# First layer's output projection in seven products of quarters (Strassen's scheme) instead of eight

## The chip, the cores and the metric

The kernel runs on one core of one Trainium2 chip. The metric is the device time in microseconds (us), the median of the runs shown. A core has a matrix engine (TensorE, in the profile PE for the matmul and PEld for loading its stationary operand), a vector engine (VectorE, DVE), a scalar engine (ScalarE, ACT), a general engine (GpSimd, POOL) and one that here only issues DMAs (SyncE, SP). Each engine works through its own list of instructions in the order in which it was built; an instruction that waits for a semaphore holds up all behind it on its engine.

## What is computed

A backbone of two layers over 512 latent tokens and 256 context tokens, 768 together, with 1024 features. Layer 0 mixes the tokens by differential attention with 8 heads, layer 1 by grouped-query attention. Cut to what the change touches, layer 0 ends so:

```python
o = rms_norm(o1 - lam * o2, subln_g) * (1 - lam_init)     # 8 heads of 128 features
y = (o.reshape(S, 1024) * silu(z)) @ w_out[0]               # the output projection
x = x + gate * rms_norm(y, post_g[0])                       # latent tokens; ctx likewise
h = rms_norm(x, pre_g[1]) * (1 + scale) + shift             # input of layer 1: K, V, Q, z
```

Below, g is the gated output of the heads (768 tokens by 1024 features), W is `w_out[0]` (1024 by 1024), and y = g W. W's quarters are W00 (heads 0 to 3, columns 0 to 511), W01 (heads 0 to 3, columns 512 to 1023), W10 and W11 (heads 4 to 7).

## The kernel before, in words

**Matmuls in three terms.** All large products are done in `fp32r` with a high and a low part of each operand: `mm3` (lines 142 to 145) issues high x high, high x low, low x high into one accumulation. An operand of 128 x 1024 weights is made by `wsplit` (line 209): a load of 512 KB into one of two "raw" buffers (line 211), a cast to the high part on ScalarE (line 213), and the difference to the low part (line 207, in `pieces`), on VectorE in one instruction or on GpSimd in four pieces of 256 columns. `WStream` (from line 225) holds the list of all weights in the order of use: a weight is asked for as soon as a slot for its two parts is free, three slots of the pool `wp`, and later one more in the pool `bp`, which lies where head 7's buffers were (`ws.extend`, line 1169). `release` frees a slot and asks for the next in the list.

**The projection.** It runs over column groups `OUTC` (line 267): 0 to 255, 256 to 511, 512 to 1023, with 2, 2 and 4 weight tiles. For each group and each of the six tiles of 128 tokens, `out_proj` (line 404) adds up eight heads of three terms: 24 matmuls with the token tile stationary and 256 or 512 columns of weights moving.

**Order of the work.** `flow` (line 346) merges the attention's steps (scores `S_`, transposes `T_`, probabilities times values `M_`, sub-layer norms `X_`) with a queue `fillq` of projections, by a planner with a cost and a due time for each step. Steps run at a raised priority, which moves their instructions ahead in the engines' lists. For head h, the norm of the head (`subln`) and `z_proj` (line 841) end in `gate_mul` (line 836), which multiplies the head by its gate on GpSimd. The last entry of the queue is `out_early` (line 1076): when seven heads are done, `split_g` (line 1023) makes high and low parts of heads 0 to 6, and the first column group is started on six banks of PSUM with the heads 0 to 6. Head 7 is finished in two parts, tokens 0 to 511 and 512 to 767, by `subln_last` (line 986), with its own gate and split (lines 998 and 999). After it the pool of layer 0 is closed, and the code from line 1165 on places new tiles there; x and the context are loaded again for the residual (lines 1171 and 1174), behind the last reader of those buffers.

The loop at lines 1206 to 1225 adds head 7 to the first group, and does the second; each tile's result is multiplied by the layer's gate (`u0`) on VectorE and squared and summed (`sumsq`) on ScalarE. The last group's loop (1274 to 1284) does the tiles of the third group, and with each of them `resid_a` (line 1230) and `resid_b` (line 1238): the norm of y, the residual and the norm of x. Two tiles later `h1_tr` (line 1255) transposes that tile on TensorE, scales it, and writes the high and low part of layer 1's input h. Then K and V of layer 1 are projected, in an order written out by hand in `KV` (line 44; loop at line 1352): 'k' and 'v' are projections, 't' the transposes of a token tile, 'c' those of K, 'g' parts of layer 1's gate vector, whose loads are `gate1_load` (line 1177). The banks of PSUM are four single ones (`bk`) and two pairs (`sc`).

## Time and profile before

| | |
|---|---|
| time before, median of 3 runs | 825.95 us (825.36 to 826.91) |
| span of the profiled execution | 822.0 us |
| median less that span | 3.95 us |
| TensorE busy in the span | 792.7 us, 96% |
| VectorE, ScalarE, GpSimd busy | 482.3, 457.1, 440.4 us |
| the stretch from 459 to 538 us (head 7's end and the projection): TensorE, VectorE, ScalarE, GpSimd busy | 76.86, 45.30, 41.91, 22.36 us |
| mean granted TensorE clock | 0.992 |

The profile shows one execution. "Busy" is the time in which an engine had an instruction at work; the span goes from the first to the last instruction. The time of a run is taken outside of it and is some microseconds longer. Of the profiled execution the page gives the span only. A row of groups reads: line of the code, engine, operation, output <- inputs, shape, count | busy time, mean in ns of one | idle time of the engine before them and who ended it. A row of waits reads: engine, line <- the one waited for: total us, times, longest.

### The profile page before, as it was taken

How to read it: one execution, taken by the hardware profiler on the slowest of the kernel's cores; microseconds unless marked ns; L12 is line 12 of the kernel's file. 1: busy time of each engine (PE TensorE's matmuls, PEld its weight loads, DVE VectorE, ACT ScalarE, POOL GpSimd, SP SyncE). 2: the span in 40 equal slices, each digit the busy share in tenths (PEclk: the TensorE clock that was granted, in tenths of full speed). 3: DMA queues.
4: the chain of work that ended last, by engine and by line, in shares of the span. 5: the costliest groups of instructions: out<-in, count | busy, mean ns of one | idle time of the engine just before them, and what ended most of it. 6: DMA issues, size and time to landing. Idle time of an engine off the chain costs nothing. (4 is left out here: it accounts for less than half of the span.)

```text
span 822.0 us, 14412 instructions
## 1 busy us (share of the span) xinstructions
PE 792.7 (96%) x5482; PEld 703.0 (86%) x5482; DVE 482.3 (59%) x896; ACT 457.1 (56%) x1001; POOL 440.4 (54%) x538
## 2 busy tenths in 40 slices
PE   7999999999999999999999999999999999999997
PEld 5678897788887898787988898889999899898986
DVE  3425566754768524675458952579546566755534
ACT  6534357664575544765556852674446576666631
POOL 4544766856367744665822311587788656733101
PEclk9999999999999999999999999999999999999999
DMA  9934211122053321323330045033421210301102
GB/s 300 347 131 142 77 39 52 52 77 90 28 154 98 122 101 65 116 78 118 113 104 26 27 151 182 1 110 103 154 79 52 78 52 1 103 26 52 50 28 103
DMA packets 41540, 77.77 MB, mean 95 GB/s; under 512 B 3584, under 2 KB 18688, under 8 KB 41472
## 3 DMA queue, kind: packets, MB, share of 16 engines
q1 hardware_dynamic: 38048, 71.71, 26.4%
q10 hardware_dynamic: 3424, 5.15, 1.8%
q8 instruction: 43, 0.70, 0.3%
q14 instruction: 25, 0.20, 0.1%
HBM read 70.56 MB, written 2.10 MB: 88 GB/s over the span
## 5 line engine op out<-in xcount | busy, mean ns | idle before, releaser
L207 POOL TENSOR_TENSOR wlo<-raw,whi 128x256 fp32r<-128x256 f32 x200 | 152.0, 792 | 72.8 <-ACT whi L213 63.1
L143 PE MATMUL bk<-whi,h 128*128 128x256 f32 (+1 forms) x592 | 176.9, 302 | 1.1 <-ACT p L1459 0.8
L144 PE MATMUL bk<-wlo,h 128*128 128x256 f32 (+1 forms) x592 | 176.2, 299 | 0.2 <-DVE wlo L207 0.2
L145 PE MATMUL bk<-whi,h 128*128 128x256 f32 (+1 forms) x592 | 175.4, 299 | 0.2 <-DVE h L1272 0.2
L143 PE MATMUL bk<-h,whi 128*128 128x512 f32 (+2 forms) x416 | 147.4, 354 | 2.7 <-ACT sq L979 1.5
L144 PE MATMUL bk<-h,whi 128*128 128x512 f32 (+2 forms) x416 | 144.8, 348 | 0.0
L145 PE MATMUL bk<-h,wlo 128*128 128x512 f32 (+2 forms) x416 | 144.8, 348 | 0.0
L143 PEld LDWEIGHTS bk<-whi,h 128*128 128x128 f32 x592 | 112.6, 191 | 8.2 <-issue 2.8
L145 PEld LDWEIGHTS bk<-whi,h 128*128 128x128 f32 x592 | 112.0, 190 | 4.7 <-issue 0.8
L144 PEld LDWEIGHTS bk<-wlo,h 128*128 128x128 f32 x592 | 112.3, 190 | 3.9 <-DVE wlo L207 0.4
L221 POOL TENSOR_SCALAR p<-p,sm 128x768 f32<-128x768 f32 (+1 forms) x80 | 67.1, 842 | 76.5 <-DVE sm L1460 28.7
L143 PEld LDWEIGHTS bk<-h,whi 128*128 128x128 f32 x416 | 78.2, 188 | 15.1 <-issue 4.0
L213 ACT CAST whi<-raw 128x1024 fp32r<-128x1024 f32 x64 | 67.1, 1048 | 36.1 <-PE bk L144 17.7
L145 PEld LDWEIGHTS bk<-h,wlo 128*128 128x128 f32 x416 | 78.3, 188 | 8.8 <-issue 1.6
L144 PEld LDWEIGHTS bk<-h,whi 128*128 128x128 f32 x416 | 78.4, 188 | 7.2 <-issue 0.8
L888 ACT ACTIVATE p<-sc,sm 128x768 f32<-128x768 f32 (+1 forms) x68 | 59.7, 881 | 37.9 <-DVE sm L885 37.9
L885 DVE TENSOR_REDUCE sm<-sc 128x1 f32<-128x768 f32 (+1 forms) x68 | 60.3, 917 | 17.4 <-PE sc L880 17.3
L181 POOL TENSOR_TENSOR sz<-sz,za 128x384 f32<-128x384 f32 (+1 forms) x24 | 28.1, 1172 | 42.8 <-ACT za L180 42.7
L896 DVE SCALAR_TENSOR_TENSOR p<-p,sm,p 128x768 f32<-128x768 f32 (+1 forms) x34 | 40.1, 1179 | 16.5 <-POOL p L221 14.9
L1480 DVE TENSOR_TENSOR al<-bk,ah 128x512 fp32r<-128x512 f32 x48 | 32.6, 687 | 26.1 <-ACT ah L1479 25.9
L950 ACT CAST ah<-bk 128x512 fp32r<-128x512 f32 x56 | 31.7, 590 | 27.9 <-PE bk L945 24.4
L880 PE MATMUL sc<-qk,qk 64*128 64x384 f32 (+1 forms) x396 | 45.8, 354 | 1.1 <-ACT p L888 1.0
(247 smaller groups left out, 1693.0 us busy)
## 6 DMA issues: line engine op xcount, KB each, us to landing
raw<-in_a_w SPq DMA_DIRECT2D x30, 512.0 KB, 3.6
araw<-in_ada_w SPq DMA_DIRECT2D x12, 1024.0 KB, 5.6
raw<-in_b_w SPq DMA_DIRECT2D x20, 512.0 KB, 3.5
ag<-in_ada_w SPq DMA_DIRECT2D x32, 256.0 KB, 6.9
raw<-in_w_out SPq DMA_DIRECT2D x16, 512.0 KB, 3.5
sw<-qr ACTq DMA_DIRECT2D x32, 128.0 KB, 2.5
gw<-in_ada_w SPq DMA_DIRECT2D x8, 512.0 KB, 3.8
xt<-in_x SPq DMA_DIRECT2D x4, 512.0 KB, 5.3
```

Of the source, the lines that this page charges most:

```text
L143: nc.tensor.matmul(o, ahi, bhi, start=start, stop=False)
L144: nc.tensor.matmul(o, ahi, blo, start=False, stop=False)
L145: nc.tensor.matmul(o, alo, bhi, start=False, stop=stop)
L207: eng.tensor_tensor(dst[:, i:i + n], a[:, i:i + n], b[:, i:i + n], op)
L213: nc.scalar.copy(hi, r)
L221: (nc.vector if eng == "v" else nc.gpsimd).tensor_scalar(dst, src, s_, 1.0, ALU.mult, ALU.mult)
L880: prev = nc.tensor.matmul(sc[m][:, j if nk == T else m, :w], a[r, tok], b[r, c], start=i == 0, stop=i == 2)
L885: nc.vector.tensor_reduce(mx, scv, AX.XY if nk == T else AX.X, ALU.max, negate=True)
L888: nc.scalar.activation(pv_, scv, AF.Exp, bias=mx, accum_out=l[:, m:m + 1])
L896: nc.vector.scalar_tensor_tensor(ps_[0], pt, r, ps_[0], ALU.mult, ALU.add)
L950: nc.scalar.copy(ah, tr)
L1480: nc.vector.tensor_tensor(al, tr, f32(ah), ALU.subtract)
```

## The change

The eight quarter products of y = g W (two halves of the tokens, two of the heads, two of the columns) are replaced by Winograd's form of Strassen's scheme with seven products, each of a half of the tokens (three tiles), four heads and 512 columns, three terms each. With token halves lo (0 to 383) and hi (384 to 767), head groups A (0 to 3) and B (4 to 7), and W's sums S2 = W01 + W11 - W00:

| product | tokens and heads | weights |
|---|---|---|
| P1 | g(lo,A) | W00 |
| P5 | T1 = g(hi,A) - g(lo,A) | W01 + W11 |
| P2 | g(lo,B) | W10 |
| P6 | T2 = g(hi,B) - T1 | S2 |
| P7 | T3 = T2 - g(lo,A) | W00 - W01 |
| P4 | T4 = g(lo,B) - T2 | W11 |
| P3 | g(hi,B) | W10 - S2 |

The products are done in this order, `PRODS`. P1 and P2 add up to y of lo, columns 0 to 511; P6, P7 and P4 are added to P1's bank in PSUM, P3 to P5's; the rest of the additions read copies of banks that are kept in SBUF (`s1`, `s5`, `u2`).

*Weights.* `wprod` (new) makes each half (two heads) of a product's weights. It loads quarters into the same two raw buffers, adds or subtracts them on the engine that `EPR` names first ('p' is GpSimd, 'v' VectorE), casts, and makes the low part on the engine named second. S2's halves stay in two tiles "xn" of the pool `bp` until P3. A product has two weight tiles; P1's and P5's go through `wp` alone, the others may use the slot in `bp`.

*Sums of tokens.* T1 is made in `gate_mul`, in place, for heads 0 to 3 (GpSimd). T2, T3 and T4 are made in place by `t_sums` after the heads are split: pairs of heads 0/4, 1/5 and 2/6 on GpSimd, the pair 3/7 on VectorE behind head 7's last split. `t_split` makes their high parts on ScalarE and the low parts on the engine that `ETS` names.

*Around it.* `out_early` does P1 and P5. The gate multiplication of the first column half goes from VectorE to GpSimd (`part`). `h1_tr` follows three tiles behind instead of two (`HL`), so three tiles of transposes are left to the K and V stage, and `KV` is ordered anew. h1's tiles are halved (`h1half`). `mm3` gets an argument that switches off the builder's check of accumulation groups, and nothing else. The core of the diff:

```diff
-KV = (('k', 0), ('k', 1), ('k', 2), ('k', 3), ('t', 4), ('v', 0), ('v', 1), ('t', 5), ('k', 4), ('c', 0), ('v', 2), ('k', 5), ('c', 1), ('g', 0), ('c', 2), ('c', 3), ('v', 3), ('g', 0), ('g', 0), ('v', 5), ('g', 0), ('c', 4), ('v', 4), ('g', 0), ('c', 5), ('g', 0), ('g', 0), ('g', 0))
+KV = (('k', 0), ('t', 3), ('v', 0), ('k', 1), ('t', 4), ('v', 1), ('k', 2), ('t', 5), ('v', 2), ('k', 3), ('c', 0), ('v', 3), ('k', 4), ('c', 1), ('c', 2), ('k', 5), ('g', 0), ('c', 3), ('v', 5), ('g', 0), ('g', 0), ('c', 4), ('v', 4), ('g', 0), ('g', 0), ('c', 5), ('g', 0), ('g', 0), ('g', 0))
+EPR = {1: ('', 'p'), 5: ('p', 'p'), 2: ('', 'v'), 6: ('pv', 'v'), 7: ('v', 'p'), 4: ('', 'p'), 3: ('v', 'v')}
+ETS = {2: 'v', 3: 'v', 4: 'p'}
+HL = 3
...
+    def wprod(half, prod, pool, slot, key):
+        def load(kq, nq):
+            r = wp.tile([P, 1024], F32, tag="raw", name=nm("raw"), bufs=2)
+            k0 = (kq * 4 + half * 2) * P
+            src = w_out[0, k0:k0 + 2 * P, nq * 512:nq * 512 + 512].rearrange("(k p) n -> p k n", p=P)
+            nc.sync.dma_start(r.rearrange("p (k n) -> p k n", k=2), src)
+            return r
+
+        es, el = EPR[prod]
+        if prod in (1, 2, 4):
+            r = load(*{1: (0, 0), 2: (1, 0), 4: (1, 1)}[prod])
+        elif prod == 5:
+            r, t = load(0, 1), load(1, 1)
+            pieces(VP[es[0]], r, r, t, ALU.add)
+        elif prod == 6:
+            a, b = load(0, 1), load(1, 1)
+            r = s2w[half] = s2_tile()
+            pieces(VP[es[0]], r, a, b, ALU.add)
+            pieces(VP[es[1]], r, r, load(0, 0), ALU.subtract)
+        elif prod == 7:
+            r, t = load(0, 0), load(0, 1)
+            pieces(VP[es[0]], r, r, t, ALU.subtract)
+        else:
+            r = load(1, 0)
+            pieces(VP[es[0]], r, r, s2w[half], ALU.subtract)
+        hi, lo = w_pair(pool, slot, key)
+        nc.scalar.copy(hi, r)
+        pieces(VP[el], lo, r, f32(hi), ALU.subtract)
+        return hi, lo
+
+    s2w = {}
+
+    def s2_tile():
+        return bp.tile([P, D], F32, tag="xn", name=nm("s2"), bufs=2)
...
+    PRODS = (1, 5, 2, 6, 7, 4, 3)
...
-    add_wout(0)
+    for key in prod_keys(*PRODS):
+        ws.add(key, key[3], key[2])
...
+    def prod_mm(o, w, kt, hi, lo, j, start=False, stop=False, more=False):
+        sl = slice(j * P, (j + 1) * P)
+        wh, wl = w[kt // 2]
+        c = slice((kt % 2) * 512, (kt % 2) * 512 + 512)
+        mm3(o, hi[:, sl], lo[:, sl], wh[:, c], wl[:, c], start, stop, more)
+        yield 3 * 512 / 2400.0
...
+                if h < 4:
+                    pieces(nc.gpsimd, gT[h][:, 384:], gT[h][:, 384:], gT[h][:, :384], ALU.subtract)
...
+            if a:
+                t_sums(3, nc.vector)
+
+        def t_sums(i, eng):
+            g, gp = gT[i], gT[i + 4]
+            lo, hi = slice(0, 384), slice(384, T)
+            pieces(eng, gp[:, hi], gp[:, hi], g[:, hi], ALU.subtract)
+            pieces(eng, g[:, lo], gp[:, hi], g[:, lo], ALU.subtract)
+            pieces(eng, gp[:, lo], gp[:, lo], gp[:, hi], ALU.subtract)
...
-            w_ = get_wout(0, *OUTC[0])
-            w_o.append(w_)
+            for i in range(3):
+                t_sums(i, nc.gpsimd)
             for ms in ((0, 1), (2, 3), (4, 5)):
                 while ms[0] == 2 and KT - 1 not in sdone:
                     yield None
                 if ms[0] < NQ:
                     sc = sc2()
-                    o_pre.extend(sc[:, j, :n] for j in range(2))
+                    o_pre.extend(sc[:, j, :] for j in range(2))
                 else:
-                    o_pre.extend(pj(n) for _ in range(2))
-                for kt in range(KT - 1):
-                    for m in ms:
-                        yield from out_proj(o_pre[m], ghi, glo, w_, m, n, kt, kt + 1)
+                    o_pre.extend(pj(512) for _ in range(2))
+                for m in ms:
+                    p = m // 3
+                    if p not in w_p:
+                        while not ws.has(*prod_keys(PRODS[p])):
+                            yield None
+                        w_p[p] = get_prod(PRODS[p])
+                    for kt in range(4):
+                        yield from prod_mm(o_pre[m], w_p[p], kt, ghi[kt][:, p * 384:], glo[kt][:, p * 384:], m % 3, kt == 0, kt == 3)
+                    if m == 2:
+                        ws.release(*prod_keys(PRODS[0]))
...
+    def h1half(n, dt=F32R):
+        return h1p.tile([P, 4, n], dt, tag="h1", name=nm("h1"), bufs=4)
...
+    tt = {p: h1half(T) for p in (2, 3, 4)}
...
+    ws.extend(bp, WX[0], [*prod_keys(*PRODS[2:]), 8, 9, 10, 11])
...
+    tops = {p: [(t[:, i, lo3], t[:, i, hi3]) for i in range(4)] for p, t in tt.items()}
+    tsrc = {2: lambda i: gT[i + 4][:, hi3], 3: lambda i: gT[i][:, lo3], 4: lambda i: gT[i + 4][:, lo3]}
+    spare = h1half(T, F32).rearrange("p a b -> p (a b)")
+    s1 = [spare[:, j * 512:j * 512 + 512] for j in range(3)]
+    s5 = [spare[:, (3 + j) * 512:(4 + j) * 512] for j in range(3)]
+    u2 = [bp.tile([P, 1024], F32, tag="gw", name=nm("u2"), bufs=2) for _ in range(2)]
+    u2 = [u2[j // 2][:, (j % 2) * 512:(j % 2) * 512 + 512] for j in range(3)]
+    b1, b5 = o_pre[:3], o_pre[3:]
+
+    def t_split(p, i):
+        hi, lo = tops[p][i]
+        nc.scalar.copy(hi, tsrc[p](i))
+        VP[ETS[p]].tensor_tensor(lo, tsrc[p](i), f32(hi), ALU.subtract)
+
+    for j in range(3):
+        nc.scalar.copy(s1[j], b1[j])
+    for i in range(3):
+        t_split(2, i)
+    for j in range(3):
+        nc.scalar.copy(s5[j], b5[j])
+
+    def part(m, k, v, src, eng):
+        if m not in ss:
+            ss[m] = small(3)
+        sumsq(ss[m][:, 0:1], src, 512)
+        nc.gpsimd.tensor_scalar(ss[m][:, 0:1], ss[m][:, 0:1], EPS, None, ALU.add)
+        u = u0[m, k] = hp.tile([P, 512], F32, tag="gT", name=nm("u0"), bufs=8)
+        eng.tensor_tensor(u, src, gate0[v][:, k * 512:k * 512 + 512], ALU.mult)
+
+    def var(m):
+        return 0 if m < NQ else 1
...
+    b21 = [(ghi[4 + i], glo[4 + i]) for i in range(4)]
+    b22 = [(ghi[4 + i][:, hi3], glo[4 + i][:, hi3]) for i in range(4)]
+    w = get_prod(2)
+    o2 = [pj(512), pj(512)]
+    for j in range(2):
+        product(o2[j], w, b21, j, range(3), True, False)
+    for i in range(3):
+        t_split(3, i)
+    for j in range(3):
+        if j < 2:
+            product(o2[j], w, b21, j, (3,), more=False)
+        else:
+            o2.append(pj(512))
+            product(o2[j], w, b21, j, range(4), True, False)
+        nc.vector.tensor_tensor(s1[j], o2[j], s1[j], ALU.add)
+        close(o2[j])
+        part(j, 0, 0, s1[j], nc.gpsimd)
+    ws.release(*prod_keys(2))
+    t_split(2, 3)
+    t_split(3, 3)
+    for i in range(4):
+        t_split(4, i)
+    w = get_prod(6)
+    for j in range(3):
+        product(b1[j], w, tops[2], j, range(3))
+    for j in range(3):
+        product(b1[j], w, tops[2], j, (3,))
+        nc.scalar.copy(u2[j], b1[j])
+    ws.release(*prod_keys(6))
+    w = get_prod(7)
+    for j in range(3):
+        product(b1[j], w, tops[3], j)
+        nc.vector.tensor_tensor(s5[j], b1[j], s5[j], ALU.add)
+        part(3 + j, 1, var(3 + j), s5[j], nc.gpsimd)
+    ws.release(*prod_keys(7))
+    h1hi, h1lo = htile1(T), htile1(T)
+    xn = {}
...
+            nc.vector.tensor_tensor(u2[m - 3], o, u2[m - 3], ALU.add)
+            if m > 3:
                 close(o)
-            if qi:
-                part_sum(ss[m])
-        ws.release(*wout_keys(0, c, n))
-    c, n = OUTC[2]
-    w = get_wout(0, c, n)
-    xn = {}
-
-    def resid_a(m, o):
-        v = 0 if m < NQ else 1
-        u1 = hp.tile([P, 512], F32, tag="gT", name=nm("u1"), bufs=8)
-        sumsq(ss[m][:, 2:3], o, n)
-        nc.vector.tensor_tensor(u1, o, gate0[v][:, c:], ALU.mult)
-        close(o)
-        xn[m] = [u1, rstd_sum(ss[m][:, 2:3], ss[m][:, 0:1])]
+            o = u2[m - 3]
+        sumsq(ss[m][:, 2:3], o, 512)
+        nc.vector.tensor_tensor(u1, o, gate0[var(m)][:, k * 512:k * 512 + 512], ALU.mult)
+        u0[m, k] = u1
+        xn[m] = rstd_sum(ss[m][:, 2:3], ss[m][:, 0:1])
...
     for i, m in enumerate(order):
-        o = pj(n)
-        run(out_proj(o, ghi, glo, w, m, n, 0, 4))
-        if i >= 2:
-            h1_tr(order[i - 2], 0)
-        run(out_proj(o, ghi, glo, w, m, n, 4, 8))
+        p, o, ops = (4, b1[i], tops[4]) if m < 3 else (3, b5[i - 3], b22)
+        if i % 3 == 0:
+            w = get_prod(p)
+        product(o, w, ops, i % 3, range(2))
+        if i >= HL:
+            h1_tr(order[i - HL], 0)
+        product(o, w, ops, i % 3, range(2, 4))
         resid_a(m, o)
-        if i >= 2:
-            h1_tr(order[i - 2], 1)
+        if i >= HL:
+            h1_tr(order[i - HL], 1)
         resid_b(m)
-    ws.release(*wout_keys(0, c, n))
+        if i % 3 == 2:
+            ws.release(*prod_keys(p))
```

Besides these, `h1_tr` and the projections that read h1 index it by halves, and layer 1's own output projection keeps its weights' list under the name `add_wout1`.

More of the change, by code (lines that the diff above doesn't have):

```diff
@@ L193, in w_off @@
         elif key[0] == "o":
[L194 removed]
+            narrow = key[1] == 1 and dict(OUTC1)[key[2]] == 256
         else:
@@ L266, in tile_backbone, with add_wout1, prod_keys, get_prod @@
     ws = WStream()
-    OUTC = ((0, 256), (256, 256), (512, 512))
+    PRODS = (1, 5, 2, 6, 7, 4, 3)
     OUTC1 = ((0, 256), (512, 512), (256, 256))
-    def add_wout(layer):
-        for c, n in (OUTC, OUTC1)[layer]:
+    def add_wout1():
+        for c, n in OUTC1:
             per = 1024 // n
             for k in range(KT // per):
-                src = w_out[layer, k * per * P:(k + 1) * per * P, c:c + n].rearrange("(k p) n -> p k n", p=P)
-                ws.add(("o", layer, c, k), src, nc.vector)
+                src = w_out[1, k * per * P:(k + 1) * per * P, c:c + n].rearrange("(k p) n -> p k n", p=P)
+                ws.add(("o", 1, c, k), src, nc.vector)
+    def prod_keys(*prods):
+        return [("o", 0, p, half) for p in prods for half in range(2)]
+    def get_prod(p):
+        return [ws.get(k) for k in prod_keys(p)]
     def wout_keys(layer, c, n):
@@ L1151, in htile1 @@
     def htile1(n):
-        return h1p.tile([P, KT, n], F32R, tag="h1", name=nm("h1"), bufs=2)
+        return [h1half(n) for _ in range(2)]
+    def h1half(n, dt=F32R):
+        return h1p.tile([P, 4, n], dt, tag="h1", name=nm("h1"), bufs=4)
     def proj_tok(o, w, t):
@@ new lines, in part, with product @@
+    def part(m, k, v, src, eng):
[7 more added lines that the diff above has]
+        return 0 if m < NQ else 1
+    def product(o, w, ops, j, kts=range(4), start=False, more=True):
+        for kt in kts:
+            run(prod_mm(o, w, kt, *ops[kt], j, start and kt == 0, kt == 3, more))
@@ L1238, in resid_b @@
     def resid_b(m):
-        u1, r = xn[m][:2]
+        r = xn[m]
         xd = x1[m] if m < NQ else (gate1, gacc)[m - NQ]
         sq = small(2)
-        for j, u in enumerate((u0[m], u1)):
+        for j in range(2):
+            u = u0[m, j]
             sl = slice(j * 512, j * 512 + 512)
```

53 lines of the change are left out of this document (18 added, 35 removed).

## The prediction

> **What bounds the kernel now.** I read the page first, then a table of windows over the end of layer 0, then TensorE's waits in that stretch, then its timeline.
>
> ```profile
> span 822.0 us, 14412 instructions
> PE 792.7 (96%) x5482; PEld 703.0 (86%) x5482; DVE 482.3 (59%) x896; ACT 457.1 (56%) x1001; POOL 440.4 (54%) x538
> ```
>
> ```profile
> core 0: us, PE busy (x) PEld busy (x) DVE busy (x) ACT busy (x) POOL busy (x), PEclk, DMA share, GB/s
> 459.00:538.00 79.00, 76.86 (x500) 68.83 (x499) 45.30 (x80) 41.91 (x108) 22.36 (x46) 1.00 0.27 96
> 546.00:549.60 3.60, 1.85 (x12) 1.15 (x11) 1.90 (x5) 3.60 (x15) 3.43 (x7) 1.00 0.72 183
> 549.60:553.40 3.80, 3.73 (x18) 3.73 (x19) 3.33 (x11) 1.71 (x10) 3.60 (x5) 0.55 0.41 143
> ```
>
> TensorE is busy 96% of the span, so a matmul that goes away is worth its time only if the next one is ready. The projection fills 459 to 538, with little idle time:
>
> ```profile
> PE sc L143 <- ACT p L888: 0.7, 1, 0.7
> PE bk L150 <- DVE al L951: 0.5, 1, 0.5
> PE sc L145 <- DVE h L1027: 0.4, 1, 0.4
> PE bk L143 <- ACT jk L1204: 0.3, 1, 0.3
> PE bk L144 <- DVE wlo L207: 0.2, 1, 0.2
> ```
>
> That is 2.1 us, and only the 0.2 is for weights. Matmuls overlap, so I price one by the distance of starts, not by its duration:
>
> ```profile
> 496.05 0.28 PE L145 MATMUL bk<-whi,h 128*128 128x256 f32 x1
> 502.43 0.28 PE L145 MATMUL bk<-whi,h 128*128 128x256 f32 x1
> 528.18 0.40 PE L143 MATMUL bk<-whi,h 128*128 128x512 f32 x1
> 534.20 0.40 PE L145 MATMUL bk<-whi,h 128*128 128x512 f32 x1
> ```
>
> 54 steps of a 256-column matmul take 6.38 us, 0.118 each; 26 steps of 512 columns take 6.02, 0.2315 each.
>
> **The change part by part.** *Matmuls.* Before: 288 of 256 columns and 144 of 512: 34.0 + 33.3 = 67.3 us. After, counted in the built program: seven products of 36 with 512 columns, 252 x 0.2315 = 58.3. Removed: **9.0 us**. The rest of TensorE's work (attention of head 7, the transposes of h1) is as before. Of the 79.0 us window, 67.3 is projection, 2.1 waiting, 24 transposes at some 0.118 are 2.8; the remaining 6.7 or so is attention.
>
> *What the weights cost now.* The other prices:
>
> ```profile
> L207 POOL TENSOR_TENSOR wlo<-raw,whi 128x256 fp32r<-128x256 f32 x200 | 152.0, 792 | 72.8 <-ACT whi L213 63.1
> L213 ACT CAST whi<-raw 128x1024 fp32r<-128x1024 f32 x64 | 67.1, 1048 | 36.1 <-PE bk L144 17.7
> raw<-in_w_out SPq DMA_DIRECT2D x16, 512.0 KB, 3.5
> ```
>
> ```profile
> L380 POOL TENSOR_TENSOR sqs<-sq,sqs 128x384 fp32r<-128x384 f32 x14 | 15.0, 1072 | 14.6 <-ACT sqs L379 12.9 <-POOL p L221 1.5
> L380 POOL TENSOR_TENSOR sqs<-sq,sqs 128x512 fp32r<-128x512 f32 x1 | 1.3, 1292 | 1.1 <-ACT sqs L379 1.1
> L207 DVE TENSOR_TENSOR wlo<-raw,whi 128x1024 fp32r<-128x1024 f32 x18 | 22.3, 1241 | 15.4 <-ACT whi L213 15.3
> L1234 DVE TENSOR_TENSOR u<-bk,gate 128x512 f32<-128x512 f32 x6 | 4.1, 688 | 10.2 <-ACT jk L1204 10.2
> ```
>
> So a full-width sum or low part (four pieces) is 3.2 us on GpSimd and 1.24 on VectorE, a cast 1.05 on ScalarE, a load 3.5 from issue to landing. Before there are 8 loads, 8 casts, 8 subtractions. After there are 22 loads (P5, P7 two per half, P6 three), 14 casts, 14 low parts and 10 sums, through the same two "raw" buffers and few weight slots. A sum of two loads holds both buffers until it is done, so the third load of P6 can't be asked for before. That turns preparation into a chain.
>
> *Order.* I followed the built program's queues, with what each instruction waits for. TensorE's order is the same up to the z projection of head 7, which ends near 459 (first row below). In GpSimd's queue four things stand in a row that matter: (1) twelve T-sum pieces and P5's sums stand ahead of the scaling of the last attention tile; (2) after P5, `u0` for P2's three tiles and the four low parts of T4 stand ahead of both `s2` sums, W12+W22 of P6; (3) the second half's `s2` sum stands behind the first's, whose buffers it needs; (4) low parts of P7, P4 follow. In SyncE's queue the second load for the first `s2` stands behind six loads of x and xc, which wait until head 7 is gated.
>
> *Before P6.* A 192-column T-sum piece isn't in the trace; between nothing and the 0.79 of 256 columns I take 0.57, near half of the 384-column row.
>
> ```profile
> 458.98 0.33 PE L145 MATMUL bk<-h,wlo 128*128 128x384 f32 x1
> 459.54 2.69 DVE L1027 TENSOR_TENSOR h<-gT,h 128x768 fp32r<-128x768 f32 x3
> 469.67 0.48 POOL L221 TENSOR_SCALAR p<-p,sm 128x256 f32<-128x256 f32 x1 [1.19 <-DVE sm L891]
> 474.25 0.49 PE L945 MATMUL bk<-ident,p 128*128 128x128 f32 x3
> 484.81 0.42 DVE L998 TENSOR_TENSOR gT<-gT,sz 128x256 f32<-128x256 f32 x1
> 485.26 0.41 ACT L999 CAST h<-gT 128x256 fp32r<-128x256 f32 x1 [0.95 <-DVE gT L998]
> ```
>
> This scaling ends 470.15. In the new queue it follows (from the fifth split of g, 462.3) 12 T pieces 6.8, P5's low part 3.2, another scaling 0.5, sz 1.2 and four sum pieces 3.2: about 477.5. TensorE, through P1 and half of P5, wants its result at 476.5: a wait of 1.7 (it may be nothing, if the pieces are short, or 3). Behind it come the low part of P5's second half 0.55, P2's cast and the bank of the last attention tile 1.6, the norm's logarithm that frees a bank 0.6, P2's second half, whose weight slot lies where head 7's buffers were (gate 0.4, cast 0.4, cast 1.05: 1.5; low part 0.8), and the bank of P2's first tile, freed by VectorE behind T splits, 1.05. Together **+7.8**, with 0 and 12 as bounds. P2 then ends near 500 (459.3 + 108 x 0.2315 + 6.7 + 1.9 old waits + 7.8).
>
> *P6.*
>
> ```profile
> 485.37 1.76 SPq L1171 DMA_DIRECT2D x<-in_x  x4
> 488.24 0.45 SPq L211 DMA_DIRECT2D raw<-in_w_out  x1
> DMA to landing us min/median/max: 3.5/4.7/11.1
> ```
>
> Behind the x loads a weight load took up to 11.1 us. The new one is issued near 494 and lands near 505, which isn't what decides: GpSimd starts `u0` at 498.4, when the first P2 tile is added up, and needs 3 x 1.29 + 4 x 1.02 + 0.8: until 507. Then sum 3.2, third load 3.5, VectorE 1.24, cast 1.05: the first P6 matmul at 516 instead of 500. **+16.2.** The second half asks for a load when VectorE has read the buffer (515.0): 3.5, sum 3.2, load 3.5, 1.24, 1.05: 527.5. TensorE has 12 matmuls until 519.7: **+7.8**, and 0.8 for the low part. P6 ends 533.8.
>
> *P7.* Its second load is asked for at 526.4: 3.5 + 1.24 + 1.05 + low part: +0.6. The next half's second load must wait for that low part (535.4): 3.5 + 1.24 + 1.05 gives 541.2 against 537.2: **+4.0**, low part +1.1. From there TensorE leads: P4 has no sum, P3's one sum on VectorE +1.2. Sum from P6 on: **31.7**.
>
> *Clock.* In 546 to 549.6 TensorE stood still for half of the window; then the granted clock is 0.55 for 3.8 us, and 18 matmuls took what 18 x 0.118 = 2.1 us would do: 1.7 lost. After, three gaps are longer. Two of the slow spells end in another wait; the third is felt: **+1.7** (0 to 5).
>
> [...]
>
> *K and V of layer 1.*
>
> ```profile
> PE sc L1261 <- POOL wlo L207: 1.3, 1, 1.3
> PE sc L1261 <- ACT hf L1269: 0.3, 1, 0.3
> PE bk L145 <- DVE h L1272: 0.2, 1, 0.2
> ```
>
> Three tiles of h1 instead of two are left to them, and VectorE arrives with a backlog of `u`, residuals and low parts: waits of 0.3 + 1.0 + 2.5 by the same adding up, against 1.8 before. **+2** (0 to 5). What it does to the early part of GpSimd's queue (a 384-column subtraction for each of heads 0 to 3) I cost at nothing: TensorE's projections hide them; uncovered they are 4 x two pieces of 0.57, 4.6.
>
> **Sum:** -9.0 + 7.8 + 31.7 + 1.7 + 2.0 = +34. Span 822.0 + 34 = 856; the median 825.95 is 3.95 above the profiled span (what lies around it), so **860**.
>
> **Rivals.** *A, weights hidden.* If P6 and P7 were ready in time, only the matmuls and small waits are left: -9 + 0 to 3, 817 to 820. For it: GpSimd was busy 22 of 79 us, VectorE 45, so there is room in sum. Against it: the room is not used in order; the sums wait behind `u0`, which waits for P2. *B, part of the chain is hidden*: the waits before P6 vanish (-7.8), and P6 is late by its shortest chain from P2's end, 0.7 + 1.3 + 0.5 + 2.8 + 3.5 + 1.2 + 1.05 = 11 instead of 16, with the P7 wait halved: 838 to 846, and less if the order of GpSimd's queue binds less than I read. It decides if the T pieces take under 0.3. [...] That the change doesn't do what it says is excluded for the matmul count, which the built program shows.
>
> **How the numbers follow.** Forecast 847 to 868, at 860: 0.70. A: 0.08. B: 0.14, of which half above 838. C above 868: 0.06, most of it below 872. No difference: 0.02. The range 838 to 872 leaves out the other half of B, A, and a little. Faster by over 0.2% (which is about what a measurement can tell from no change) 0.08, within 0.2% 0.02, slower 0.90.
>
> **What would show it.** In the profile after: a TensorE wait of over 10 us whose releaser is the cast of `s2` (P6's first half), a second of 6 to 9 on the next cast, a third near 4 on P7's second half; GpSimd standing idle before `u0`; loads of w_out one after another at 3.5 us with SyncE waiting for GpSimd and VectorE between them; 252 matmuls of 512 columns at 0.23. Wrong if TensorE's largest wait between P2 and K is under 3 us, or if it waits for T splits or banks instead of weights.

## The result, and the profile after

The changed kernel takes **884.57 us** (median of 4 runs, 883.34 to 885.23) against 825.65 in the same sitting: 1.0716 times as long, 95% interval 1.0699 to 1.0734. The forecast was 860.0 (838 to 872): the sign and the largest wait (P6's weights) were right, the size was not. The profiled execution spans 883.4 us, 61.4 more than before; below, differences of one profile to another are differences of spans.

The page of the changed kernel, its first lines:

```profile
span 883.4 us, 14192 instructions
...
PE 803.3 (91%) x5302; PEld 698.9 (79%) x5302; DVE 510.0 (58%) x908; ACT 473.3 (54%) x1016; POOL 506.3 (57%) x616
```

180 matmuls fewer (432 went, 252 came), yet TensorE is busy 10.6 us longer. One reason is the half clock: where the granted clock is 0.50 (474.2 to 477.6) a matmul of 512 columns shows 0.63 us in the timeline and the next starts 0.43 later, against 0.40 and 0.23 where it is 1.00. Below, the first finished row is the first tile of 128 tokens of which y is complete in all columns; its time is the start of the gating that reads it. The largest of TensorE's waits from 462 us to the first finished row (571.6):

```profile
PE sc L146 <- ACT whi L246: 25.4, 3, 17.2
PE bk L999 <- DVE p L950: 9.2, 1, 9.2
PE sc L146 <- ACT p L942: 1.9, 1, 1.9
```

The longest of TensorE's idle times in the same stretch of its timeline, each in brackets before the instruction that ended it:

```profile
490.29 0.90 PE L999 MATMUL bk<-ident,p 128*128 128x128 f32 x3 [9.18 <-DVE p L950]
...
529.80 1.22 PE L146 MATMUL sc<-whi,h 128*128 128x512 f32 x2 [17.25 <-ACT whi L246]
...
541.26 1.22 PE L146 MATMUL sc<-whi,h 128*128 128x512 f32 x2 [5.57 <-ACT whi L246]
...
555.08 0.74 PE L146 MATMUL sc<-whi,h 128*128 128x512 f32 x2 [2.62 <-ACT whi L246]
```

The second is P6's first half, the third its second half, the fourth P7's second half. GpSimd's queue ahead of P6 stands as it was read, the loads' sums behind `u0`:

```profile
518.40 1.26 POOL L1306 TENSOR_TENSOR u<-h,gate 128x512 f32<-128x512 f32 x1
519.74 0.48 POOL L1304 TENSOR_SCALAR sm<-sm 128x1 f32<-128x1 f32 x2
520.28 2.76 POOL L210 TENSOR_TENSOR s<-raw,raw 128x256 f32<-128x256 f32 x4
532.29 2.78 POOL L210 TENSOR_TENSOR s<-raw,raw 128x256 f32<-128x256 f32 x4 [9.25 <-DMA raw<-in_w_out]
```

The wait of 9.18 us was not foreseen. GpSimd's timeline beside it, and VectorE's:

```profile
481.30 0.48 POOL L259 TENSOR_SCALAR p<-p,sm 128x256 f32<-128x256 f32 x1
481.74 0.59 POOL L210 TENSOR_TENSOR gT<-gT,gT 128x192 f32<-128x192 f32 x1
...
487.20 2.76 POOL L210 TENSOR_TENSOR wlo<-raw,whi 128x256 fp32r<-128x256 f32 x4
```

```profile
481.81 8.42 DVE L950 SCALAR_TENSOR_TENSOR p<-p,sm,p 128x256 f32<-128x256 f32 x1 [7.53 <-POOL p L259]
```

GpSimd works without a pause from the scaling's end to 489.96; VectorE's addition starts at 481.81 and ends at 490.23, though it waits for nothing but that scaling. In the kernel before, the same addition took 1.46, beside GpSimd's sum for the norm, and the one before it, of the same shape, 0.47:

```profile
471.31 1.46 DVE L896 SCALAR_TENSOR_TENSOR p<-p,sm,p 128x256 f32<-128x256 f32 x1
```

Windows around these waits; the columns are those of the table of windows in the prediction, the granted clock third from the end:

```profile
474.20:477.60 3.40, 3.40 (x10) 2.61 (x9) 0.08 (x1) 0.00 (x0) 3.40 (x7) 0.50 0.09 30
...
490.30:494.70 4.40, 4.40 (x15) 3.57 (x16) 2.36 (x3) 2.32 (x4) 0.14 (x1) 0.50 0.00 0
...
529.80:535.60 5.80, 5.76 (x12) 3.63 (x12) 1.20 (x1) 0.00 (x0) 2.78 (x4) 0.50 0.26 88
541.30:545.90 4.60, 4.56 (x10) 3.16 (x11) 2.39 (x2) 0.79 (x1) 0.00 (x0) 0.50 0.33 115
```

P6's first 12 matmuls take 5.8 us, with a short wait for their low part, where 12 x 0.2315 would be 2.8.

**Where the time went.** The distances between the starts of all matmuls, added up in the trace, against their steps at full clock (0.118 for 256 columns, 0.2315 for 512). The first stretch goes from the same matmul of head 7 (459.1 before, 461.9 after) to the first finished row:

| to the first finished row | before | after |
|---|---|---|
| matmuls at full clock | 48.8 | 54.0 |
| TensorE's idle times over 0.25 us | 1.9 | 41.5 |
| the rest (half clock, short gaps) | 2.0 | 14.2 |
| sum | 52.8 | 109.7 |

That is 56.9 of the 61.4; 2.8 were there already at 462, and 1.7 come behind. So behind the first finished row the kernel gained nothing from the shorter projection. The gating by VectorE, with the shortest, median and longest in ns, and the first and last start in us (the rows of before, then of after):

```profile
L1234 DVE TENSOR_TENSOR u<-bk,gate x6: 678/691/692, 511.9 to 540.0; 128x512 f32<-128x512 f32 x6
```

```profile
L1362 DVE TENSOR_TENSOR u<-sc,gate x3: 678/683/693, 571.6 to 582.7; 128x512 f32<-128x512 f32 x3
L1362 DVE TENSOR_TENSOR u<-u,gate x3: 682/685/686, 589.9 to 591.1; 128x512 f32<-128x512 f32 x3
```

From the first of them to the end it is 822.0 - 511.9 = 310.1 before and 883.4 - 571.6 = 311.8 after.

### The profile page after: what moved, and what is told of

Same layout as the page of the kernel before. It is cut to its first block, busy times and chain, and to the rows that moved or that the text cites. A ratio compares the mean times of both kernels' runs of the same rounds, so it can differ in the third digit from the quotient of the medians.

```text
span 883.4 us, 14192 instructions
## 1 busy us (share of the span) xinstructions
PE 803.3 (91%) x5302; PEld 698.9 (79%) x5302; DVE 510.0 (58%) x908; ACT 473.3 (54%) x1016; POOL 506.3 (57%) x616
## 4 chain that ended last, share of the span: by engine, by line
PE 63%; POOL 14%; DVE 9%; DMA 5%; ACT 4%; issue 3%; SPq 1%; POOLq 0%; DVEq 0%; ACTq 0%
PE bk L146 12%; PE bk L147 12%; PE bk L148 12%; PE bk L153 7%; POOL wlo L210 5%; PE sc L934 4%; DMA raw<-in_w_out 2%; PE bk L999 2%; PE sc L146 2%; PE sc L147 2%; PE sc L148 2%; PE bk L1606 2%; PE bk L788 1%; POOL p L259 1%; DVE p L950 1%
## 5 line engine op out<-in xcount | busy, mean ns | idle before, releaser
L210 POOL TENSOR_TENSOR wlo<-raw,whi 128x256 fp32r<-128x256 f32 x232 | 177.1, 794 | 98.9 <-ACT whi L216 66.1
L146 PE MATMUL bk<-whi,h 128*128 128x256 f32 (+1 forms) x508 | 152.0, 303 | 8.2 <-DVE vl L1503 4.7
L147 PE MATMUL bk<-wlo,h 128*128 128x256 f32 (+1 forms) x508 | 151.7, 300 | 1.5 <-DVE wlo L210 1.2
L148 PE MATMUL bk<-whi,h 128*128 128x256 f32 (+1 forms) x508 | 150.5, 299 | 2.7 <-DVE h L1401 2.7
L146 PEld LDWEIGHTS bk<-whi,h 128*128 128x128 f32 x508 | 97.7, 193 | 16.1 <-DVE vl L1503 5.2
L148 PEld LDWEIGHTS bk<-whi,h 128*128 128x128 f32 x508 | 96.8, 192 | 6.8 <-DVE h L1401 3.3
L147 PEld LDWEIGHTS bk<-wlo,h 128*128 128x128 f32 x508 | 97.4, 192 | 5.1 <-DVE wlo L210 2.1
L146 PEld LDWEIGHTS bk<-h,whi 128*128 128x128 f32 x416 | 78.2, 188 | 14.2 <-issue 3.7
L216 ACT CAST whi<-raw 128x1024 fp32r<-128x1024 f32 x56 | 58.6, 1046 | 44.3 <-PE bk L147 13.4
L146 PE MATMUL sc<-whi,h 128*128 128x512 f32 (+1 forms) x88 | 35.2, 410 | 32.0 <-ACT whi L246 25.4
L950 DVE SCALAR_TENSOR_TENSOR p<-p,sm,p 128x768 f32<-128x768 f32 (+1 forms) x34 | 46.4, 1366 | 21.3 <-POOL p L259 19.7
L1004 ACT CAST ah<-bk 128x512 fp32r<-128x512 f32 x56 | 31.7, 590 | 35.6 <-PE bk L999 31.7
L146 PEld LDWEIGHTS sc<-whi,h 128*128 128x128 f32 x88 | 18.5, 214 | 37.6 <-ACT whi L246 27.0
```

The source lines that it names most:

```text
L146: nc.tensor.matmul(o, ahi, bhi, start=start, stop=False, skip_group_check=more)
L147: nc.tensor.matmul(o, ahi, blo, start=False, stop=False, skip_group_check=more)
L148: nc.tensor.matmul(o, alo, bhi, start=False, stop=stop, skip_group_check=more)
L210: eng.tensor_tensor(dst[:, i:i + n], a[:, i:i + n], b[:, i:i + n], op)
L216: nc.scalar.copy(hi, r)
L950: nc.vector.scalar_tensor_tensor(ps_[0], pt, r, ps_[0], ALU.mult, ALU.add)
```

## The experiments

Times are medians beside the kernel before on the same chip (825.0 to 826.5). Most kernels have two runs; the seven plain products have four, the half of the last group ten, the last two four and seven, and each of the two kernels with an added block one, of which only the block's durations are used.

**T sums on VectorE.** `t_sums(i, nc.gpsimd)` becomes `t_sums(i, nc.vector)`.

> The T sums of three head pairs go from GpSimd to VectorE, nothing else. Theory (GpSimd's stream of T pieces first delays the last scaling of p and then holds up VectorE's last addition L950, which took 8.42 us): TensorE's wait of 9.18 for that addition falls under 1.5 us, the addition takes under 1.5, the half-clock spell behind it goes, and the time falls by 7 to 11 us, to 874 to 878. Rival (the 8.42 us come from something else than GpSimd's work, such as a late event): the wait stays above 5 us and the time within 3 us of 884.6.

882.46 us. The addition takes 0.48 and its wait falls from 9.18 to 1.23, but VectorE, which now has the sums, is late twice for L1005 (4.5 us together). P6 starts 6.4 us earlier, and in the end the span is 2.8 shorter; the time forecast was missed. That the T pieces are needed for the 8.42 us is confirmed; the move has its own price.

**First sum of P6 on VectorE.** `6: ('pv', 'v')` becomes `6: ('vv', 'v')`.

> Only the first sum of P6's weights (W01 + W11) goes from GpSimd to VectorE. Theory (this sum stands behind u0 and T4's low parts in GpSimd's queue, and the third load waits for it): the first wait of P6, 17.25 us, falls by 5 to 8, the second, 5.57, by 1 to 2, the time to 874 to 879. Rival (the loads themselves, late behind those of x, set P6's start, whoever adds): waits and time within 2 us of the changed kernel's.

874.48 us; P6's waits are 10.94 and 4.28. As expected: the sum's place in GpSimd's queue, not the loads, held the third load.

**Staged loads.**

```diff
-            a, b = load(0, 1), load(1, 1)
+            a, b, c = (load(*q, t) for q, t in zip(((0, 1), (1, 1), (0, 0)), stage[half]))
...
-            pieces(VP[es[1]], r, r, load(0, 0), ALU.subtract)
+            pieces(VP[es[1]], r, r, c, ALU.subtract)
...
+    stage[0], stage[1] = [x1[0], x1[1], x1[2]], [x1[3], gate1, gacc]
```

(The loads of x and the context stand behind P6's release.)

> P6's six loads go into the buffers of x, gate1 and gacc, and the loads of x and the context are asked for behind P6 instead; with it the scheduler puts the sums of P6 ahead of u0. Theory (two raw buffers turn load, sum, load, subtraction into a chain): P6's first wait 17.25 falls to 4 to 7, its second, 5.57, to under 2, P7's 2.6 and 0.8 to about nothing, the spells of half clock in P6 shrink to one; time 858 to 866. Rival (GpSimd and VectorE haven't the throughput for the sums in this stretch): the sum of the waits from P6 to P7 falls by less than 8 us, and the time stays above 875.

869.69 us. P6's waits: 4.80, then 4.12 for its low part, 0.45 and 0.29, 9.7 instead of 22.8. That is more than the sum's place alone brought, which left 10.94 and 4.28; but here GpSimd also does P6's first sum ahead of `u0`, so the two buffers are not priced apart. The time is 4 us over the forecast; the 4.12 for VectorE's low part was not in it.

**VectorE's addition beside GpSimd, in a block by itself.** Behind the end of the kernel before (for each kind of block; n pieces of w columns):

```diff
+                nc.gpsimd.tensor_scalar(lq, lp, 0.5, 1.0, ALU.mult, ALU.mult)
+                for _ in range(n):
+                    nc.gpsimd.tensor_tensor(lg[:, :w], lq[:, :w], lg[:, :w], ALU.subtract)
...
+                    nc.vector.scalar_tensor_tensor(lp, lq, lr, lp, ALU.mult, ALU.add)
```

> The kernel before, with blocks on scratch tiles added behind its end; the output is unchanged. In each block GpSimd scales a 128x256 tile, VectorE adds to it, and GpSimd goes on with 14 pieces of 128x192 (or none, or 4 of 256) on another tile. Theory (an addition on VectorE with two inputs in SBUF is held up by GpSimd's stream): the addition takes about 0.5 us alone, 3 to 9 us beside the 14 pieces, and about 0.5 beside them when one input is in PSUM. Rival (it only waits for the piece under way, or not at all): 0.5 to 1.1 us in all blocks.

0.42 to 0.49 us in all blocks: the rival. But here each piece depended on the one before, VectorE started first, and GpSimd's first piece was the slower one (0.88 instead of 0.59; beside an input in PSUM 0.59). So the block was repeated with independent pieces:

> Blocks behind the end of the kernel before, as in the first port run, but the 14 pieces that follow on GpSimd do not depend on the tile that VectorE reads, nor each on the one before it, and so follow without gaps, as the T pieces did (the last block kind has 8 of 128 columns). Theory (GpSimd, once it has begun its stream, holds VectorE's two-input addition off until the stream pauses): the addition takes 6 to 9 us with both inputs in SBUF and about 0.4 with one in PSUM. Rival (VectorE gets in at the end of the piece under way): 0.5 to 1.2 us.

The timeline of that run, first beside pieces of 192 columns, then with an input in PSUM, then beside pieces of 128:

```profile
823.74 1.31 POOL L1625 TENSOR_TENSOR lg<-lg,lg 128x192 f32<-128x192 f32 x2
823.81 0.80 DVE L1627 SCALAR_TENSOR_TENSOR lp<-lq,sm,lp 128x256 f32<-128x256 f32 x1 [0.52 <-POOL lq L1621]
...
840.16 1.13 POOL L1625 TENSOR_TENSOR lg<-lg,lg 128x192 f32<-128x192 f32 x2
840.23 0.42 DVE L1631 TENSOR_TENSOR lp<-bk,lq 128x256 f32<-128x256 f32 x1 [7.41 <-POOL lq L1621]
...
848.19 3.33 POOL L1625 TENSOR_TENSOR lg<-lg,lg 128x128 f32<-128x128 f32 x8
848.26 3.54 DVE L1627 SCALAR_TENSOR_TENSOR lp<-lq,sm,lp 128x256 f32<-128x256 f32 x1 [7.61 <-POOL lq L1621]
```

Both cases exist: 0.80 beside two pieces that take 1.31, as if let in at the end of the first, or held until the whole stream is over (3.54 beside 3.33 of GpSimd). With one input in PSUM it took 0.42. What decides between the first two stays open; that the addition can be held through many instructions (here eight) is shown. Neither forecast covers both.

**T sums later.** The same pieces stay on GpSimd, queued behind its low part for head 7's last norm:

```diff
             if a:
+                with tc.issue_after(g.ins):
+                    for i in range(3):
+                        t_sums(i, nc.gpsimd)
                 t_sums(3, nc.vector)
```

> The 18 T-sum pieces stay on GpSimd but are queued behind its low part for head 7's last norm, so that nothing of them lies beside the last scaling of p and VectorE's last addition. Theory (the stream of pieces caused both the late scaling and the addition of 8.42 us): the addition takes under 2 us, TensorE's wait for it falls from 9.18 to under 1.5, without the waits for VectorE that the move of the sums there had brought; time 871 to 876. Rival (the sums are needed where they stood): a new wait of over 4 us for T2's split appears ahead of P6, and the time stays within 4 us of 884.6.

877.35 us. The addition takes 1.22, TensorE waits 0.64 for it: the T pieces again, now without a new wait over 2 us ahead of P6. 7 us come back, a little less than forecast.

**TensorE kept busy.** 18 matmuls ahead of P6 and 9 ahead of its second half, `nc.tensor.matmul(dm, ident, gate0[0][:, :512])`.

> 27 matmuls of 512 columns on the gate, into a bank that nobody reads, are put ahead of P6 (18) and ahead of its second half (9), to keep TensorE busy through the waits for weights; the output is unchanged. Theory (P6's two halves are paced by the weights' chain and not by TensorE, so that the slow first half only shortens the wait for the second): the clock stays at full speed from 512 to 550, but the time falls by 1 to 3 us only, to 881 to 884, and the wait ahead of the second half grows. Rival (each half-clock spell adds its loss to the time): 4.5 to 6 us less, 878 to 880.

Its windows, against 0.86 and 0.64 in the changed kernel:

```profile
462.00:512.00 50.00, 34.76 (x153) 26.15 (x152) 34.16 (x45) 25.62 (x55) 28.49 (x39) 0.90 0.30 108
512.00:550.00 38.00, 35.48 (x100) 19.43 (x98) 8.40 (x8) 6.36 (x12) 14.79 (x20) 0.96 0.36 116
```

885.48 us (883.78 to 887.17): no gain, and neither forecast of the time. The filler also took more than was meant (15.6 and 7.9 us in the timeline), so that P6's second half starts at 542.33, behind it, though its cast ends at 539.60. But the weights came no sooner for the faster first half: P6's first cast ends 1.6 us earlier than in the changed kernel (528.10 against 529.74), and that of P7's second half 1.5 (553.55 against 555.02). So in P6 the half clock only fills a wait that the weights cause anyway, as forecast.

**Staged loads and late sums.**

> Both edits: staged loads for P6, and the T sums behind head 7's last norm. If the two causes add up: 869.7 less the 10 to 13 us of the late scaling, the held addition and the half clock behind it, 857 to 861. If the earlier start only lengthens P6's wait for its loads (which wait for head 7's last gating in any case): 864 or more.

863.57 us, between the two cases: 6.1 less than staged loads alone.

**Seven products without their preparation.** `wprod` loads one plain quarter; all sums of tokens are left out.

```diff
+        r = load(*{1: (0, 0), 5: (0, 1), 2: (1, 0), 6: (0, 1), 7: (0, 1), 4: (1, 1), 3: (1, 0)}[prod])
...
-            if a:
-                t_sums(3, nc.vector)
...
```

> Seven products of the same size and order, but each from one plain quarter of the weights (one load, no sum), and without any sum of tokens; the output is therefore not the reference's. It prices the matmuls alone. Theory (the seven products save 9.0 us of TensorE, and what was lost is the preparation of their operands): TensorE's waits from 459 to the start of K fall from 46 us to 3 to 6, K starts near 532 (538 before), and the time is 818 to 826, the rest being the K and V stage. Rival (the reshaped projection itself is slow, by its banks, its backlog on VectorE or its order): above 832.

**842.33 us** (841.64 to 845.44), 1.0202 of before (1.0185 to 1.0219): the rival. Without any sum, the seven products are still 16.7 us slower. They are not the matmuls alone: 14 weight tiles instead of 8 are loaded, cast and split, the copies and additions of banks are kept, and so is what else the change did (the order of `KV`, transposes three tiles behind, the gating on GpSimd). No run takes these apart. The idle times ahead of the first finished row are 8.6 us, none over 1.8. Its gating and its windows ahead of and behind the first finished row:

```profile
L1341 DVE TENSOR_TENSOR u<-sc,gate x3: 685/692/692, 528.1 to 540.7; 128x512 f32<-128x512 f32 x3
```

```profile
461.90:528.10 66.20, 57.65 (x255) 44.55 (x253) 36.63 (x53) 39.30 (x79) 37.79 (x44) 0.97 0.36 125
528.10:609.90 81.80, 69.10 (x468) 64.25 (x468) 61.91 (x116) 44.47 (x123) 56.50 (x83) 0.90 0.37 114
```

The first finished row is 16.2 us later than before, of which 2.8 are there already at 461.9. From there to the same matmul of layer 1 (1500 before the end) it is 81.8 us; in the kernel before it is 78.7, with more matmuls in it:

```profile
511.90:590.60 78.70, 76.08 (x525) 70.10 (x524) 57.18 (x112) 42.83 (x122) 54.84 (x80) 0.98 0.29 90
```

**Plain weights, all sums of tokens.** Only `wprod` is as above.

> As the seven plain products, but with all sums of tokens kept; the output is not the reference's. Theory (two separate causes): the held addition with its wait of 9 us and the half clock behind it stay, the waits of P6 and P7 go: 846 to 858, that is 25 to 35 us from the weights and the rest, over the kernel with seven plain products, from the sums of tokens. Rival (the sums of tokens cost little once the weights are there): within 6 us of the kernel with seven plain products.

848.26 us, which lies in both forecasts; but the premise of the first is gone, since the addition is not held here:

```profile
479.68 0.81 DVE L935 SCALAR_TENSOR_TENSOR p<-p,sm,p 128x256 f32<-128x256 f32 x1 [3.69 <-POOL p L244]
```

GpSimd's stream behind the scaling is not shorter than in the changed kernel: the same T pieces and other instructions in the same order, without a pause from 479.60 to 491.19. So the T pieces beside the addition do not suffice to hold it; why they don't here stays open. The sums of tokens cost 5.9 us over the seven plain products, and the sums of the weights with their loads, and the held addition, 36.3.

**Order of the last tiles.** `order = (2, 0, 1, 3, 4, 5)`.

> In the last loop the tiles go in the order 2, 0, 1, 3, 4, 5, so that the tile which shares a pair of PSUM banks with P3's first tile is read out first. Theory (the wait of 4.25 us at 583 for L1362 is for that shared pair, and the half-clock spell behind it follows from it): the wait falls under 1.5, and the time to 878 to 881. Rival (VectorE's backlog is what is late, whichever bank): the wait stays over 3 us or turns up at the next transposes, time within 2 us of 884.6.

886.35 us: the rival. The wait of 4.25 is gone, and the transposes wait 11.1 for the scaling of h1 (L1398) instead.

**All mends.**

> Staged loads, T sums behind head 7's last norm, the first sum of P6 on VectorE, and tile 2 first. If the parts add up: 863.6 less about 5 for the order of tiles and 1 to 3 for the sum, 855 to 858. If VectorE, which now has every sum of the weights, becomes the late one in P6: 860 to 864. No theory expects it under 826.

861.96 us. This is the second case. The two further mends add 1.6 us to staged loads and late sums, not 6 to 8; the largest waits are now 5.4 us for VectorE's addition L1329 and 10.6 for the scaling of h1.

**The kernel before with half of its last group.**

```diff
-        run(out_proj(o, ghi, glo, w, m, n, 0, 4))
+        run(out_proj(o, ghi, glo, w, m, n, 0, 2, 4))
...
-        run(out_proj(o, ghi, glo, w, m, n, 4, 8))
+        run(out_proj(o, ghi, glo, w, m, n, 2, 4, 4))
```

(The last argument is the head behind which the accumulation closes.)

> The kernel before, whose last column group adds up four heads instead of eight: 72 matmuls of 512 columns less, 16.7 us, right ahead of and between the norms of layer 0's result; everything else stays, the output is not the reference's. Theory (from the first finished tile on, the chain of norm, residual, norm, transposes and split of six tiles takes some 55 us on VectorE, ScalarE and GpSimd, whatever TensorE does beside it): it starts only 2.8 us earlier, and the time falls by 2 to 7 us, to 819 to 824. Rival (TensorE sets the pace here, as its 96% suggest): 14 to 17 us less, 809 to 812.

**824.61 us against 825.04**, ratio 0.9984 (0.9970 to 0.9998). 16.7 us of matmuls less gain 0.4: even the theory had expected more. 60 of the 72 matmuls, 13.9 us, lie behind the first finished row, which comes 4.0 us earlier.

```profile
span 822.9 us, 14257 instructions
...
PE 783.4 (95%) x5410; PEld 694.2 (84%) x5410; DVE 484.7 (59%) x896; ACT 459.2 (56%) x1001; POOL 440.2 (54%) x538
```

```profile
507.90:591.10 83.20, 70.44 (x478) 64.43 (x477) 59.16 (x115) 43.62 (x122) 57.54 (x85) 0.94 0.31 98
```

The last projection is done earlier, K starts 16.0 us earlier (522.0), and then TensorE waits for h1 (5.0 us), for the normed K (3.0) and others, until all is given back at 591. The granted clock is lower in this stretch (0.94; 0.98 before), but that isn't where the time went: three runs of the half group with a mean clock of 0.993 to 0.995 took 823.48 to 824.64 us too.

**Tile by tile.** In the seven plain products and in the mended kernel (staged loads, late sums, first sum on VectorE), TensorE's order in P7, P4 and P3 is fixed (`tc.issue_after`), with P4's first tile ahead of P7's last.

> The seven plain products, with TensorE's order in P7, P4 and P3 fixed tile by tile and P4's first tile ahead of P7's last; the output is not the reference's. The scheduler had spread P4 over its three tiles, so that the first was finished with the last. Theory (the chain of the tiles, counted from the first finished tile, sets the end): the first gating of P4's result comes 6 to 9 us earlier against the start of P7, and the time falls from 842.3 to 833 to 838. Rival (banks or the order of K and V set the end): 840 or more.

> Staged loads, T sums behind head 7's last norm, the first sum of P6 on VectorE, and P7, P4 and P3 tile by tile with P4's first tile ahead of P7's last (tiles in the order 0 to 5). By the same theory 5 to 9 us less than the 863.6 of staged loads and late sums alone: 854 to 859. Rival (VectorE, which has the weights' sums as well, is late for each tile): 861 or more.

844.12 (842.06 to 846.17) and 864.26 us: no gain that can be measured, so the rival in both. The first finished row came only 3.0 us earlier in the first (525.1) and 0.5 in the second (547.1). TensorE now waits in P7 and P4 for the readers of the banks: 2.1 us for ScalarE's copies and 1.7 for VectorE's additions in the first, 5.9 for VectorE's in the second.

**Work shifted off and onto VectorE** in the kernel before: `HFD = 0` and `HFD = 4` instead of 2.

> The kernel before, with all four scalings of each transposed quarter row of h1 on ScalarE instead of two on VectorE (HFD 0): 24 of 0.36 us leave VectorE, 24 of 0.40 come to ScalarE, between the first finished row and layer 1's K and V. Theory A (VectorE's work paces the stretch of some 80 us behind the first finished row): 3 to 8 us faster. Theory B (no single engine does, but each row's way through ScalarE, GpSimd, VectorE and TensorE): within 3 us of the kernel before, and not faster on both sides of it.

> The kernel before, with all four scalings on VectorE (HFD 4): 24 of 0.36 us more for VectorE. Theory A: 3 to 8 us slower. Theory B: within 3 us.

830.97 and 829.86 us, 1.0062 (1.0042 to 1.0081) and 1.0065 (1.0042 to 1.0088): slower on both sides, by more than the 3 us expected. VectorE alone doesn't pace the stretch.

**All together.** The first gating of a finished row, the end of the span, and the distance:

| kernel | first row | end | distance |
|---|---|---|---|
| before | 511.9 | 822.0 | 310.1 |
| half of the last group | 507.9 | 822.9 | 315.0 |
| seven plain products | 528.1 | 843.4 | 315.3 |
| the same, tile by tile | 525.1 | 839.9 | 314.8 |
| staged loads, late sums | 547.6 | 861.9 | 314.3 |
| staged loads | 554.3 | 867.6 | 313.3 |
| first sum on VectorE | 562.9 | 873.5 | 310.6 |
| changed kernel | 571.6 | 883.4 | 311.8 |

The first row moves over 64 us and the distance by 5; in the other runs of the whole kernel it lies between 311.9 and 316.2. This is a correlation, and the half group itself goes against reading it as a cause: its first row came 4.0 us earlier, and the end did not. That matmuls behind the first row count for next to nothing in the kernel before is shown directly by the half group.

## Why the prediction was wrong, point by point

- **"Removed: 9.0 us."** The count was right (252 of 512 columns at 0.2315), its worth was not. This is the step that failed in kind: the sum took the 9.0 in full, as if TensorE set the pace at every place of the projection. But the first finished row now needs 192 matmuls of 512 columns, 44.4 us, where it needed 288 of 256 and 24 of 512, 39.6: the change puts 4.9 us more ahead of it, and takes 13.9 away behind it, where in the half group 16.7 us less (13.9 of them behind the row) were worth 0.4. Rival A, with all weights hidden, forecast 817 to 820; without any sum of weights or tokens 842.33 was measured.
- **Before P6, +7.8.** P2 ended at 512.4 and not near 500, 2.8 of it from ahead of 462. The T pieces took 0.58 us as assumed (0.57); what failed was to price only the scaling's place in the queue. The addition behind it took 8.42 instead of 1.46, and the wait was 9.18 where 1.7 stood; with the T pieces on VectorE or later, the wait was 1.23 and 0.64. The other waits of this part (0.36 to 1.9) are as small as they were put.
- **P6 and P7, 31.7.** 17.25 against 16.2, 5.57 against 7.8, then nothing against 0.6 and 3.4 (2.62 and 0.75) against 5.1: 26.2 measured, and the causes as named (the sum behind `u0`; the two raw buffers, which were not priced apart). P3's weights cost 0.65 where 1.2 stood, and the 1.02 taken for a low part of T4 is 1.07 in its row. The mechanism was right, and the sum a little over what came.
- **Clock, +1.7.** Mis-sized: half clock and short gaps are 12.2 us more ahead of the first finished row. In P6 it is swallowed, as said (the run with TensorE kept busy gains nothing); what the spells at 474, 490 and in P7 cost was not tested apart. The time came out above 868, where C stood for more time at the half clock: spells of 3.4 to 20.5 us are there, but nothing shows that they make up the difference.
- **K and V, +2.** K starts 50.1 us later (588.2 against 538.1) and the end is 61.4 later: 11.3 more. The prediction counted waits of the same kind as before, 3.8 against 1.8; behind K's start TensorE now waits 4.7 us for V's low part on VectorE (L1503), which is not among the waits of before, and 2.7 for h1. The stretch behind the first row keeps its length of about 80 us, so the matmuls taken away there bring nothing: the 9.3 us over the forecast are about the 9.0 that the sum had taken off. That they are the same is argued, not shown.
- **"I cost at nothing"** the subtractions of T1 in heads 0 to 3: 2.8 us late at 462, of which 1.0 is there from 190 us on. A step of 0.9 near 190 us is in each profile with these subtractions and in none without them, so this is their price. The rest fits a half-clock spell at 433.2, which profiles of the kernel before (half group, `HFD = 4`) show as well.

So of the missing 27 us in the span, 12 lie ahead of P6, about 9 behind the start of K, and 11 in between, in the clock and in P3's wait for a bank (4.25), while the waits of P6 and P7 came out 5.5 shorter. What paces the 80 us stays open: in the kernel before TensorE is busy 76.08 of 78.7 us there, yet with matmuls taken away the stretch gets no shorter and no engine is full (in the half group's 83.2 us the fullest are TensorE with 70.4 and VectorE with 59.2). VectorE alone is excluded; a chain through all four is argued, not shown.

## What to carry to other kernels

A high busy share doesn't make an engine the bound (TensorE was busy 96% of the span before, and 16.7 us of matmuls less gained 0.4): remove some of its work at the place in question, and look whether the end moves. For a projection that is followed by a norm, count the matmuls ahead of the first complete row apart from those behind it: here the scheme saved work behind it, where it bought next to nothing, and added some ahead. That the first row alone sets the end is not shown. And a stream of short GpSimd instructions on SBUF can hold a two-input addition on VectorE as long as the stream lasts (3.54 us beside 3.33 of pieces in the block by itself, 8.42 in the changed kernel); it did so in five of the six kernels that had the T pieces beside the addition.

## What the runs showed of the hardware

- VectorE's addition with both inputs in SBUF took 8.42 us in the changed kernel, which has the T pieces beside it and P5's sums ahead of it on GpSimd; in the four others with both (first sum of P6 on VectorE, staged loads, TensorE kept busy, order of the last tiles) TensorE waited 8.34 to 10.76 for it, against 9.18. It took 0.81 with the T pieces and without those sums, 0.48 with the T sums on VectorE, 1.22 with the T sums later, and 1.46 in the kernel before. In the block with independent pieces it took 0.48 alone, 0.80 beside pieces of 192 columns, 3.54 beside pieces of 128, and 0.42 with one input in PSUM. A wait for the piece under way would cost at most some 0.6 more (an estimate from the pieces' 0.59); the 0.80 and 0.81 fit it, the 3.54 through eight instructions and the 8.42 through a dozen do not.
- In the changed kernel the granted clock was 0.50 in spells of 3.4 us (from 474.2), 6.8 (from 539.1), 10.2 (from 484.4) and 20.5 (from 515.2), the first of them behind an idle time of only 1.89 us (471.6 to 473.5). An idle time of that order is not always followed by one: behind 1.58 us, up to 432.35, the changed kernel has a spell (0.51 from 433.2 to 436.6), and behind 1.57, up to 431.38, the kernel before has none (1.00 from 431.4 to 440).
